# A hybrid decoder step on one core: page rows of 512 in two rings, chain loads one step ahead, operands of all products at equal places, and an end of its own for the last tile

## The chip, the core and the metric

The kernel runs on one core of a Trainium2 chip. The metric is the device time of one execution in microseconds (us). The engines are TensorE (PE in the rows of the profile, PEld for its weight loads), VectorE (DVE), ScalarE (ACT) and GpSimd (POOL); SyncE (SP) issues most of the DMAs. Matrices wait in SBUF, 128 partitions wide; TensorE writes its sums into PSUM. In a matmul one operand is loaded and stays (the stationary one, 128x128), the other streams through (the moving one, up to 512 columns).

## What is computed

One layer of a decoder over 16 meta tokens and 2048 prompt tokens, and over 8 running sequences of 4 tokens each. Two branches read the same projection: a diagonal state space layer (S5) and a gated DeltaNet (an attention with a matrix state, worked in chunks). Gates merge them, an output projection and a gated feed-forward layer follow, each with a norm and a residual. Cut to its core:

```python
hn = rms_norm(x, lp['norm_mix_pre'])
proj = hn @ lp['w_in']                                   # 1024 x 4616
u, qkv, z, a, bt, gates = jnp.split(proj, [o1, o2, o3, o4, o5], axis=-1)
y_s5, h_re_n, h_im_n = s5_mix(u, ...)                    # scan of a complex diagonal state
gs = jax.nn.gelu(y_s5)
br_a = (gs @ lp['w_s5_glu_a']) * jax.nn.sigmoid(gs @ lp['w_s5_glu_b'])
qkv_c, conv_new = short_conv(qkv, conv_buf, lp['gdn_conv_w'])
...
o_seg, S = gdn_segment(q, k, v, g, beta, S)              # chunks: decay, triangular solve, state
o = rms_norm(o, lp['gdn_norm']) * jax.nn.silu(zf)
br_b = o @ lp['w_gdn_out']
mix = (jax.nn.sigmoid(ga) * br_a + jax.nn.sigmoid(gb) * br_b) @ lp['w_out']
x = x + rms_norm(mix, lp['norm_mix_post'])
f = rms_norm(x, lp['norm_ffn_pre'])
f = (jax.nn.silu(f @ lp['w_ffn_gate']) * (f @ lp['w_ffn_up'])) @ lp['w_ffn_down']   # 1024 -> 2816 -> 1024
x = x + rms_norm(f, lp['norm_ffn_post'])
```

## The kernel before

All is float32. A product of two float32 matrices is made of three faster ones: each operand is split into a high and a low part (type fp32r), and `mm3` (L156 to L161) adds high x high, high x low and low x high, so every product is a run of three matmuls per 128 rows of the contraction.

The 2048 tokens stand in four blocks of 512; block 0 also carries the 16 meta tokens and the 32 sample tokens (560 columns, `PW`). The stages follow each other in time:

- **First stage** (`p1`, 0 to 1280 us of the page's span). `p1_features` loads the tokens of a block in tiles of 128, normalises them, transposes them on TensorE (`to_features`, `pst` at L252) and writes the features of the block, split in two, into *pages*: `pages(4)` takes four tiles of two rows for the high part (`pgh`) and four for the low one (`pgl`), each row 560 columns, out of one pool of 16 tiles. Blocks 0 and 1 form the first half, blocks 2 and 3 the second. In each half 36 units of 128 output columns of `w_in` (4 u, 12 qkv, 20 gates) multiply their weights (stationary, `wu`) with the pages (moving): `psq` and `psg`, eight rows of the contraction x three matmuls. Weights come through `wload` (L142 load, L144 high part on ScalarE, L146 and L147 low part, one half each on GpSimd and VectorE). Beside the units, by a count of ticks, run the S5 setup and groups, and the chunks of the DeltaNet: `gdn_alpha` loads a chunk's keys transposed (`kTa`, L584) and its decays (`E`, L562), multiplies keys with keys (`psk`, L590) and stores a chunk matrix (`m_d<-Z`, L607); all three tiles share three buffers (tag `al`). `gdn_chunk` solves and updates the state: `px` (L740) is a product of two times four small matmuls, with a copy to SBUF (`X`, L750) after each four; `o_out` normalises a chunk's output and transposes it (`pT`, L732). `s5_setup` loads the rows of the matrix C for half of the 32 groups (`ctl`, L1021) and transposes them (L1044).
- **Merge** (`merge`, 1280 to 1596): `p2_prep` multiplies and splits into pages again (two tiles for each of four lists), `p2_products` makes three products of each of 8 column tiles per block (`psgb`, `psga`, `psgo`; contraction of 4 rows).
- **Way out** (`way_out`, 1596 to 1800): the product with `w_out`. Here the merged rows (`hh`, and the low part) are stationary and the weights move; 17 tiles of tokens. The old rows x come into one pool of three buffers (`tm`).
- **Gate and up** (`gate_up`, 1800 to 2697): the two widest products (`psf`, 348 columns), untouched by the change.
- **Down** (`down`, 2697 to 3215): the product with `w_ffn_down`, in two halves of 8 token tiles, four groups of 5 or 6 weight tiles each. `hh` and `hl` (the split activations) are stationary, the weight tiles move (`psr` L1652 to L1655), sums are added up in `facc` (L1659). When the last group is done, a tile is normalised (Square on ScalarE L233, a root, a scaling L1666) and a GpSimd DMA adds it into `y_prompt` in memory (L1669), where the residual already stands.

Order: the program is Python that issues instructions in turn; a scheduler then lays them out in a fixed order for each engine, and each engine runs its own list from the front. A wait at the head of a list holds all behind it. SP's list holds nearly all loads and stores of a stage. Tiles of one tag share a fixed number of buffers: a new tile waits until the oldest is no longer read. Pools take their memory one after the other, from the left or the right end of SBUF, so a tile's size sets where the next pools' tiles start. The pool order of the down stage is `cv3`, `lw`, `hr`, `hh`, `ac3` from the left; `lw` has one buffer of 4096 bytes a partition.

What the edits touch in the text: `to_features` L243, `gdn_alpha` L573, `o_out` L711, `gdn_chunk` L737, `s5_setup` L881, `pages` L1246, `p2_prep` L1250, `way_rows` L1357, `down_tiles` L1630, the pools in `run` L1685, `p1_features` L1835.

## Time and profile before

| | us |
|---|---|
| time, median of 3 runs | 3237.43 (3235.34 to 3238.28) |
| the profiled execution | 3230.07 |
| its span in the profile | 3228.3 |
| first stage, its first half and its second | 0 to 722, 722 to 1280 |
| merge, way out | 1280 to 1596, 1596 to 1800 |
| gate and up, down, the end | 1800 to 2697, 2697 to 3215, 3215 to 3228 |
| mean granted clock of TensorE | 0.978 of full speed |

The profile is of one execution. A row of its timeline has the start and the duration of an instruction, the engine, the line, the operation, `out<-in` by the program's names and the shape; in brackets, how long the engine was idle ahead of it and what released it. A matmul's duration overlaps that of its neighbours, since matmuls are pipelined. A row of the waits has the engine, what it could not start, what released it, then the idle time in all, the number of waits and the longest. A row of a stretch of time has its length, busy time and number of instructions of each engine, the granted clock, the share of the DMA engines' time and GB/s. `issue` is idle time with no wait that the profile shows.

### The profile page before, as it was taken

What the parts mean: (1) busy time and instruction counts of PE and PEld (TensorE: products, weight loads), DVE (VectorE), ACT (ScalarE), POOL (GpSimd) and SP (SyncE); (2) the same over time, 40 slices, a digit from 0 to 9 for tenths busy, and PEclk for the clock granted to TensorE, in tenths of its full rate; (3) what the DMA queues carried; (4) which work ended last, traced back from release to release, by engine and by line L of the source; (5) the groups of instructions that cost most, each with busy time, mean ns of one, the idle gap of its engine ahead of it and who ended that gap; (6) DMA issues with size and microseconds to landing.
All of it is one profiled execution on the core that took longest, in us unless ns stands there. A gap on an engine that the chain in (4) does not pass through costs nothing.

```text
span 3228.3 us, 47504 instructions
## 1 busy us (share of the span) xinstructions
PE 3095.1 (96%) x17461; PEld 2719.5 (84%) x17461; DVE 2047.1 (63%) x4674; ACT 1127.2 (35%) x1952; POOL 892.9 (28%) x907
## 2 busy tenths in 40 slices
PE   7998989999999999899999899999999999999998
PEld 6887887877777887888788799999999998887776
DVE  6888864557798645644456777777777773245235
ACT  4642222433333224311244444444444444223211
POOL 1133431113332211300211444434434444121110
PEclk9999998999999999999999999999999999999999
DMA  4335556445556645544555533343323335235214
GB/s 120 122 98 164 137 157 179 116 111 141 158 172 180 169 120 149 173 132 134 162 175 190 171 105 105 105 123 106 105 88 105 105 105 174 83 107 133 88 57 70
DMA packets 460552, 419.29 MB, mean 130 GB/s; under 512 B 112330, under 2 KB 384906, under 8 KB 460320
## 3 DMA queue, kind: packets, MB, share of 16 engines
q1 hardware_dynamic: 450048, 382.18, 40.6%
q0 software_dynamic: 10272, 34.09, 3.8%
q8 instruction: 137, 2.24, 0.3%
q14 instruction: 95, 0.78, 0.1%
HBM read 288.27 MB, written 127.65 MB: 129 GB/s over the span
## 4 chain that ended last, share of the span: by engine, by line
PE 67%; DVE 15%; issue 10%; DMA 5%; ACT 2%; POOL 1%; SPq 0%; POOLq 0%; DVEq 0%; ACTq 0%
PE psf L161 9%; PE psf L159 9%; PE psf L160 9%; PE psr L1652 3%; PE psr L1653 3%; PE psr L1655 2%; PE psg L159 2%; PE psg L161 2%; PE psg L160 2%; DVE cy L391 2%; PE psr L1377 2%; PE psr L1378 2%; PE psr L1380 1%; PE psq L159 1%; PE psq L161 1%
## 5 line engine op out<-in xcount | busy, mean ns | idle before, releaser
L159 PE MATMUL psf<-xh,ah 128*128 128x348 f32 (+1 forms) x1848 | 595.0, 322 | 6.2 <-ACT sn L1546 4.5
L160 PE MATMUL psf<-xl,ah 128*128 128x348 f32 (+1 forms) x1848 | 593.8, 321 | 0.0
L161 PE MATMUL psf<-xh,al 128*128 128x348 f32 (+1 forms) x1848 | 593.5, 321 | 0.0
L146 POOL TENSOR_TENSOR wu<-wr,wu 128x512 fp32r<-128x512 f32 x136 | 218.1, 1606 | 690.0 <-ACT wu L144 664.1
L159 PEld LDWEIGHTS psf<-xh,ah 128*128 128x128 f32 x1848 | 348.3, 188 | 8.0 <-ACT sn L1546 5.4
L161 PEld LDWEIGHTS psf<-xh,al 128*128 128x128 f32 x1848 | 348.4, 189 | 0.2 <-DVE al L1486 0.2
L160 PEld LDWEIGHTS psf<-xl,ah 128*128 128x128 f32 x1848 | 348.4, 189 | 0.0
L159 PE MATMUL psg<-pgh,wu 128*128 128x512 f32 (+2 forms) x800 | 301.2, 377 | 1.2 <-ACT gt L1223 1.2
L1652 PE MATMUL psr<-wu,hh 128*128 128x512 f32 (+2 forms) x748 | 295.9, 396 | 3.9 <-ACT hh L1638 3.9
L1653 PE MATMUL psr<-wu,hh 128*128 128x512 f32 (+2 forms) x748 | 295.8, 395 | 0.0
L161 PE MATMUL psg<-pgh,wu 128*128 128x512 f32 (+2 forms) x800 | 290.3, 363 | 4.0 <-DVE wu L147 4.0
L160 PE MATMUL psg<-pgl,wu 128*128 128x512 f32 (+2 forms) x800 | 289.2, 362 | 0.0
L1655 PE MATMUL psr<-wu,hl 128*128 128x512 f32 x704 | 277.3, 395 | 0.0
L147 DVE TENSOR_TENSOR wu<-wr,wu 128x512 fp32r<-128x512 f32 x136 | 121.0, 891 | 130.7 <-ACT wu L144 127.8
L144 ACT ACTIVATE wu<-wr 128x1024 fp32r<-128x1024 f32 x136 | 142.6, 1054 | 133.8 <-DMA wr<-w_ffn_down 48.8
L159 PE MATMUL psq<-pgh,wu 128*128 128x512 f32 (+2 forms) x480 | 183.1, 381 | 4.6 <-ACT gt L1223 4.0
L161 PEld LDWEIGHTS psg<-pgh,wu 128*128 128x128 f32 x800 | 156.0, 195 | 28.7 <-DVE wu L147 4.2
L159 PEld LDWEIGHTS psg<-pgh,wu 128*128 128x128 f32 x800 | 155.8, 195 | 26.6 <-issue 6.1
L160 PE MATMUL psq<-pgl,wu 128*128 128x512 f32 (+2 forms) x480 | 174.4, 363 | 0.0
L161 PE MATMUL psq<-pgh,wu 128*128 128x512 f32 (+2 forms) x480 | 173.7, 362 | 0.0
L1652 PEld LDWEIGHTS psr<-wu,hh 128*128 128x128 f32 (+2 forms) x748 | 138.8, 186 | 39.8 <-ACT hh L1638 4.2
L160 PEld LDWEIGHTS psg<-pgl,wu 128*128 128x128 f32 x800 | 155.9, 195 | 19.2 <-issue 0.2
(498 smaller groups left out, 6721.3 us busy)
## 6 DMA issues: line engine op xcount, KB each, us to landing
wr<-w_in SPq DMA_DIRECT2D x72, 512.0 KB
araw<-w_ffn_gate SPq DMA_DIRECT2D x31, 1024.0 KB
araw<-w_ffn_up SPq DMA_DIRECT2D x31, 1024.0 KB
wr<-w_ffn_down SPq DMA_DIRECT2D x44, 512.0 KB
zg_d<-gt SPq DMA_DIRECT2D x80, 256.0 KB
h_d<-hm SPq DMA_DIRECT2D x44, 348.0 KB
qkv_d<-cy SPq DMA_DIRECT2D x48, 256.0 KB
hr<-h_d SPq DMA_DIRECT2D x16, 768.0 KB
```

Source lines behind the costliest of these rows:

```text
L144: nc.scalar.activation(hi[:, :n], raw[:, :n], AF.Copy)
L146: nc.gpsimd.tensor_sub(lo[:, :c], raw[:, :c], hi[:, :c].bitcast(F32))
L147: nc.vector.tensor_sub(lo[:, c:n], raw[:, c:n], hi[:, c:n].bitcast(F32))
L159: t.matmul(ps, wh, xh, start=first, stop=False, **kw)
L160: t.matmul(ps, wh, xl, start=False, stop=False, **kw)
L161: t.matmul(ps, wl, xh, start=False, stop=last, **kw)
L391: nc.vector.scalar_tensor_tensor(yp, raw[:, j:j + np_], w[j], yp, op0=OP.mult, op1=OP.add)
L1377: nc.tensor.matmul(o, hi[:, k, :rr], wh[:, cs], start=i == 0, stop=False)
L1378: nc.tensor.matmul(o, hi[:, k, :rr], wl[:, cs], start=False, stop=wide and i == 7)
L1652: nc.tensor.matmul(ps, hi[:, k, cl], wh[:, cs], start=k == 0, stop=False)
L1653: nc.tensor.matmul(ps, hi[:, k, cl], wl[:, cs], start=False, stop=both and k == n - 1)
L1655: nc.tensor.matmul(ps, lo[:, k, c - c0:c - c0 + r], wh[:, cs], start=False, stop=k == n - 1)
```

## The change

- **Pages.** One block's pages are now units of eight rows: a unit for the high part and one for the low part in the first stage; in the merge both parts of a list stand in one unit. There are two rings (`pg0` for even blocks, `pg1` for odd ones) of two units each. A row has 512 columns (2048 bytes), in block 0 it has 576 (`PITCH`, 2304 bytes); before, every row had 560 (2240 bytes).
- **First tokens.** In block 0, `to_features` takes three of its four PSUM tiles from the pool `gp` in place of `pt`.
- **Loads ahead.** `gdn_alpha` issues a chunk's `kTa` and `E` one chunk earlier; the tag `al` has five buffers in place of three. `s5_setup` issues the rows of C earlier (`rows_c`), into a buffer of the token tiles `tm` in place of `cv`.
- **Small moves.** `px`: both copies now come behind all eight matmuls. `o_out`: one more step of the count ahead of `pT`. The way out's x tiles go to three tags in a fixed turn, one buffer each. The down stage's twelve weight buffers come from two pools of six.
- **Operand places.** `lows`, in `lw`, has 96 columns more (4480 bytes for 4096), so all that lies behind it in the down stage (`hr`, `hh`, `ac`) starts 384 bytes later modulo 512.
- **The end.** The last prompt tile of the down stage has a path of its own (`down_end`): its residual is loaded ahead, the sum of squares and the scaling are made in two halves, and two plain SP stores write the result.

The diff, cut (line 41 adds `PITCH = 576`; `p1_features` passes `b == 0` as `wide`):

```diff
@@ -240,13 +241,14 @@
-    def to_features(self, ys, gain, hi, lo):
+    def to_features(self, ys, gain, hi, lo, wide):
 
         nc = self.nc
         c0 = ys[0][2]
         w = sum(r for _, r, _ in ys)
         for k0 in range(0, 8, 2):
-            ps = self.pt.tile([P, 2, 256], F32, tag="pt", name="pst")
+            pool, tag = (self.gp, "gp") if wide and k0 else (self.pt, "pt")
@@ -578,11 +580,15 @@
         v.memset(ssk, 1.0)
-        zs = []
+        new = lambda nm: self.gd.tile([P, H, P], F32, tag="al", bufs=5, name=nm)
+        def load(ci, nt, c0):
+            kT = new("kTa")[:, :, :nt]
+            nc.sync.dma_start(kT, ap_of(self.qkv_d, 512 * QW + c0, [[QW, P], [P * QW, H], [1, nt]]))
+            return kT, self.decay_load(ci, nt, new("E"))
+        nxt = load(*ch[0])
         for i, (ci, nt, c0) in enumerate(ch):
-            kT = self.gd.tile([P, H, P], F32, tag="al", bufs=3, name="kTa")[:, :, :nt]
-            nc.sync.dma_start(kT, ap_of(self.qkv_d, 512 * QW + c0, [[QW, P], [P * QW, H], [1, nt]]))
-            e = self.decay_load(ci, nt, self.gd.tile([P, H, P], F32, tag="al", bufs=3, name="E"))
+            kT, e = nxt
+            nxt = load(*ch[i + 1]) if i + 1 < n else None
@@ -592,7 +598,7 @@
-            z = self.gd.tile([P, H, P], F32, tag="al", bufs=3, name="Z")[:nt, :, :nt]
+            z = new("Z")[:nt, :, :nt]
@@ -726,6 +732,7 @@
         yield
+        yield
         pT = self.gp.tile([P, H, P], F32, tag="gp", name="pT")
@@ -747,6 +754,7 @@
                 mm(px[a:a + 32, h, 0:32], M[a + 32:a + 64, h, a:a + 32], V[a + 32:a + 64, h])
+        for a in (0, 64):
             v.tensor_copy(X[a:a + 32], px[a:a + 32, :, 0:32])
@@ -998,6 +1006,13 @@
 
         nc.sync.dma_start(ld[:16], ap_of(io["s5_D"], 0, [[1, 16], [16, G]]))
+        def rows_c(h0):
+            t = self.tm.tile([P, D], F32, tag="tm", name="ctl")[:, :512].rearrange("p (i q k e) -> p i q k e", i=2, q=2, k=2)
+            for i, nm in enumerate(("s5_C_re", "s5_C_im")):
+                for k in range(2):
+                    nc.sync.dma_start(t[:, i, :, k], ap_of(io[nm], h0 * 16 * 64, [[64, P], [P * 64, 2], [1, 64]]))
+            return [t[:, i] for i in range(2)]
+        nxt = rows_c(0)
 
@@ -1014,12 +1029,7 @@
             for d, nm in ((Br, "s5_B_re"), (Bi, "s5_B_im")):
                 for sl in (lo, hi):
                     nc.sync.dma_start(d[sl], io[nm].rearrange("o g p c -> p (o g) c")[:, h0:h0 + 16])
-            cts = []
-            for nm in ("s5_C_re", "s5_C_im"):
-                ct = self.c2("ctl")[:, :256].rearrange("p (q k e) -> p q k e", q=2, k=2)
-                for k in range(2):
-                    nc.sync.dma_start(ct[:, :, k], ap_of(io[nm], h0 * 16 * 64, [[64, P], [P * 64, 2], [1, 64]]))
-                cts.append(ct)
+            cts = nxt
@@ -1071,6 +1081,8 @@
                 outer(V2, (CR, CI), (R2, R1), "n", 1, 9)
+                if g0 == 12:
+                    nxt = rows_c(16)
                 nc.sync.dma_start(self.wv_d[gs, :, 3].rearrange("g p (t c) -> p g t c", c=16), V2)
@@ -1243,16 +1255,26 @@
 
-    def pages(self, n):
-        new = lambda nm: [self.pg.tile([P, 2, PW], F32R, tag="pg", name=nm) for _ in range(n)]
-        return new("pgh"), new("pgl")
+    def pages(self, b, n):
+
+
+        pitch = PITCH if b == 0 else BLK
+        out = []
+        for nm in ("pgh", "pgl"):
+            if n == 4 or nm == "pgh":
+                t = self.pg.tile([P, 8 * (PITCH if b % 2 == 0 else BLK)], F32R, tag=f"pg{b % 2}", bufs=2, name=nm)
+                rows = t[:, :8 * pitch].rearrange("p (k c) -> p k c", k=8)
+                at = 0
+            out.append([rows[:, at + 2 * i:at + 2 * i + 2] for i in range(n)])
+            at += 2 * n
+        return out
 
     def p2_prep(self, b):
 
         nc, v = self.nc, self.nc.vector
         width = BLK + SMP if b == 0 else BLK
 
-        oh, ol = self.pages(2)
+        oh, ol = self.pages(b, 2)
@@ -1364,7 +1386,8 @@
-        x = self.tm.tile([P, D], F32, tag="tm", name="xr")
+        n = c // P + 1 if c < SEQ else 0
+        x = self.tm.tile([P, D], F32, tag=f"tm{n % 3}", name="xr")
@@ -1645,6 +1669,9 @@
             cl = slice(c - c0, c - c0 + rr)
+            if gi == last and c + r == SEQ:
+                end = self.down_end(a, r, c)
+                next(end)
             for half in range(2):
@@ -1657,16 +1684,42 @@
                     v.tensor_add(a[:rr, cs], a[:rr, cs], ps)
+                if end:
+                    next(end)
             if wide and gi == last - 1:
-                t = self.lw.tile([SMP, D], F32, tag="lw", name="lows")
+                t = self.lw.tile([SMP, D + 96], F32, tag="lw", name="lows")[:, :D]
                 nc.sync.dma_start(t, a[r:2 * r])
                 nc.gpsimd.tensor_add(a[:r], a[:r], t)
-            if gi == last:
+            if gi == last and not end:
                 rs = self.rstd_of([(a, r, c)], "f")
                 v.scalar_tensor_tensor(a[:r], a[:r], rs[:r, 0:1], self.r_fpost[:r], op0=OP.mult, op1=OP.mult)
                 dst = (ap_of(self.io["y_prompt"], c * D, [[D, r], [1, D]]) if c < SEQ
                        else ap_of(self.io["y_sample"], 0, [[D, r], [1, D]]))
                 nc.gpsimd.dma_start(dst, a[:r], accum_op=OP.add)
+
+    def down_end(self, a, r, c):
+
+        nc, v = self.nc, self.nc.vector
+        rows = lambda cs: ap_of(self.io["y_prompt"], c * D + cs.start, [[D, r], [1, cs.stop - cs.start]])
+        halves = [slice(0, BLK), slice(BLK, D)]
+        y = self.lw.tile([P, D + 96], F32, tag="lw", name="yl")[:, :D]
+        nc.sync.dma_start(y, rows(slice(0, D)))
+        g = self.ac.tile([P, D], F32, tag="ac", name="fg")
+        ss = self.small.tile([P, 2], F32, tag="sse", bufs=1, name="sse")
+        rs = self.small.tile([P, 1], F32, tag="rse", bufs=1, name="rse")
+        yield
+        for i, cs in enumerate(halves):
+            j = self.c2("sq").bitcast(BF16)[:, :BLK]
+            nc.scalar.activation(j, a[:, cs], AF.Square, accum_out=ss[:, i:i + 1])
+            v.tensor_mul(g[:, cs], a[:, cs], self.r_fpost[:, cs])
+            if i == 0:
+                yield
+        v.tensor_add(ss[:, 0:1], ss[:, 0:1], ss[:, 1:2])
+        self.rsqrt(rs, ss[:, 0:1], 1.0 / D, EPS, "e")
+        for cs in halves:
+            v.scalar_tensor_tensor(g[:, cs], g[:, cs], rs[:, 0:1], y[:, cs], op0=OP.mult, op1=OP.add)
+            nc.sync.dma_start(rows(cs), g[:, cs])
+        yield
@@ -1703,7 +1756,7 @@
-                self.pg = self.pool("pg", 16, pgx, side="right")
+                self.pg = self.pool("pg", 2, pgx, side="right")
@@ -1726,7 +1779,7 @@
-                self.tm = self.pool("tm2", 3, ph, **kw)
+                self.tm = self.pool("tm2", 1, ph, **kw)
@@ -1758,7 +1811,8 @@
-            self.wp.add(self.pool("wp3", 12, ph, side="right", **kw), 12)
+            self.wp.add(self.pool("wp3", 6, ph, side="right", **kw), 6)
+            self.wp.add(self.pool("wp5", 6, ph, side="right", **kw), 6)
```

The scheduler lays out the new program anew, and in the first stage the rows of most engines have moved. Three places follow, each a piece of one engine's list before and after. Line numbers are those of the respective program (L584 is L586 after, L562 is L564, L607 is L613, L740 is L747, L159 to L161 are L160 to L162).

SP in the first stage, around the first full chunks of the DeltaNet, before. `kTa` and `E` are a chunk's loads, `m_d<-Z` its store, `zg_d<-gt` the store of a gate unit, `ctl` the rows of C, `wr<-w_in` the load of a weight tile:

```order
L1021 DMA ctl<-s_C_re 128x2x64 x2
L1021 DMA ctl<-s_C_im 128x2x64 x2
L1228 DMA zg_d<-gt 128x512
L607 DMA m_d<-Z 256x1x64
L1229 DMA zg_d<-gt 128x32
L584 DMA kTa<-qkv_d 128x4x128
L562 DMA E<-gct_d 128x512
L1231 DMA zg_d<-gt 128x512
L1068 DMA wv_d<-V 128x4x128
L142 DMA wr<-w_in 128x8x128 x2
```

The same place after:

```order
L1240 DMA zg_d<-gt 128x512
L1241 DMA zg_d<-gt 128x32
L586 DMA kTa<-qkv_d 128x4x128
L613 DMA m_d<-Z 256x1x64
L564 DMA E<-gct_d 128x512
L1243 DMA zg_d<-gt 128x512
L143 DMA wr<-w_in 128x8x128
L1078 DMA wv_d<-V 128x4x128
L586 DMA kTa<-qkv_d 128x4x128
L564 DMA E<-gct_d 128x512
L613 DMA m_d<-Z 128x512
```

Each chunk's loads now stand ahead of the store of the chunk before it, and the loads of C are gone from here. They stand near the front of SP's list, behind the stores of zeros (`L336`), ahead of the first store of a conv output (`qkv_d<-cy`), after:

```order
L218 DMA xt<-x_prompt 128x1024
L333 DMA u_d<-zero 128x4x8 x5
L336 DMA qkv_d<-zero 128x16 x12
L1013 DMA ctl<-s_C_re 128x2x64 x2
L1013 DMA ctl<-s_C_im 128x2x64 x2
L406 DMA qkv_d<-cy 128x16
L407 DMA qkv_d<-cy 128x32
L408 DMA qkv_d<-cy 128x512
```

TensorE in the first half, at the first chunk's `px` product (between the matmuls of a gate unit), before:

```order
L160 MATMUL psg<-pgl,wu 128x304
L740 MATMUL px<-U_5599,M 32x32 x4
L161 MATMUL psg<-pgh,wu 128x304
L159 MATMUL psg<-pgh,wu 128x304
L160 MATMUL psg<-pgl,wu 128x304
L161 MATMUL psg<-pgh,wu 128x304
L740 MATMUL px<-U_5599,M 32x32 x4
```

After:

```order
L160 MATMUL psg<-pgh,wu 128x304
L161 MATMUL psg<-pgl,wu 128x304
L747 MATMUL px<-U_5585,M 32x32 x8
L162 MATMUL psg<-pgh,wu 128x304
L160 MATMUL psg<-pgh,wu 128x304
L161 MATMUL psg<-pgl,wu 128x304
```

The two fours of `px`, four gate matmuls apart before, now stand together.

9 lines of the change are left out of this document (6 added, 3 removed).

## The prediction

> **What bounds the kernel now.** I read the page first, then busy time and clock by stage, the matmuls of single stretches in order of time, and PE's waits.
>
> ```profile
> span 3228.3 us, 47504 instructions
> PE 3095.1 (96%) x17461; PEld 2719.5 (84%) x17461; DVE 2047.1 (63%) x4674; ACT 1127.2 (35%) x1952; POOL 892.9 (28%) x907
> PE 67%; DVE 15%; issue 10%; DMA 5%; ACT 2%; POOL 1%; SPq 0%; POOLq 0%; DVEq 0%; ACTq 0%
> ```
>
> TensorE is busy nearly throughout and carries two thirds of the chain, so there are two ways to gain: matmuls that follow each other faster, and fewer waits of PE. The next rows give, by stretch, its length, then busy time (and count) of PE, weight loads, DVE, ACT and POOL, granted clock, DMA share and GB/s: the start, the first pass with the S5 setup, the second pass, the way out, and the down projection.
>
> ```profile
> 0.00:135.00 135.00, 110.64 (x636) 97.82 (x637) 102.68 (x356) 76.43 (x140) 17.46 (x22) 0.95 0.42 118
> 135.00:430.00 295.00, 266.98 (x1624) 235.42 (x1622) 246.69 (x853) 100.03 (x191) 107.85 (x121) 0.95 0.47 133
> 722.00:1020.00 298.00, 287.56 (x1369) 231.88 (x1368) 242.56 (x769) 96.47 (x191) 94.69 (x182) 0.98 0.56 160
> 1596.00:1800.00 204.00, 200.66 (x940) 162.52 (x941) 123.50 (x306) 85.51 (x157) 36.35 (x52) 1.00 0.55 181
> 2697.00:3215.00 518.00, 515.14 (x2210) 411.25 (x2210) 209.68 (x389) 123.63 (x143) 88.45 (x59) 1.00 0.38 102
> ```
>
> In the down projection PE never waits, so its time is its number of matmuls times their spacing. In the first 430 us PE is idle for 52 us in all, and VectorE is busy for 349 of 430: there a wait of PE may hide a VectorE that is nearly as late.
>
> **The matmuls' spacing.** A row's own duration (0.39 us) overlaps its neighbours', so I take starts. All these matmuls are 128x512, at full granted clock. Way out, first and last of 19 that follow each other; then the down projection (52), the merge (25) and the last gates of the first stage (11):
>
> ```profile
> 1678.77 0.39 PE L1377 MATMUL psr<-wu,hh 128*128 128x512 f32 x1
> ...
> 1682.85 0.39 PE L1377 MATMUL psr<-wu,hh 128*128 128x512 f32 x1
> ```
>
> ```profile
> 2907.01 0.39 PE L1652 MATMUL psr<-wu,hh 128*128 128x512 f32 x1
> ...
> 2918.86 0.39 PE L1652 MATMUL psr<-wu,hh 128*128 128x512 f32 x1
> ```
>
> ```profile
> 1459.91 0.39 PE L159 MATMUL psgo<-pgh,wu 128*128 128x512 f32 x1
> ...
> 1465.46 0.39 PE L159 MATMUL psga<-pgh,wu 128*128 128x512 f32 x1
> ```
>
> ```profile
> 1245.24 0.39 PE L160 MATMUL psg<-pgl,wu 128*128 128x512 f32 x1
> ...
> 1247.55 0.39 PE L161 MATMUL psg<-pgh,wu 128*128 128x512 f32 x1
> ```
>
> That is 4.08 us over 18 steps or 226.7 ns in the way out, 11.85 over 51 or 232.4 ns in the down projection, 5.55 over 24 or 231.3 ns in the merge, 2.31 over 10 or 231.0 ns in the gates. The way out and the down projection run the same three products in the same order. What differs in the built program is where the operands start: in the way out moving and stationary tiles both lie at 480 bytes modulo 512; in the down projection the moving weights lie at 480 and the stationary tiles at 96; in the merge and the first stage the stationary ones lie at 480 and the moving page rows wander, row by row, by 192 or 448 bytes modulo 512. The change puts all of them at 480, but for the odd rows of the first block (224). I read the 226.7 ns as the price of equal places.
>
> - Down: 2210 matmuls x 5.7 ns = 12.6 us. Nothing else stands on that path, so all of it counts.
> - Merge: blocks 1 to 3, 8 columns x 3 products x 4 k x 3 matmuls each = 864, x 4.6 ns = 4.0 us. All of it counts, since PE is the bound here too.
> - First stage: 36 units x 3 blocks x 24 = 2592, x 4.3 ns = 11.1 us. I count 6: in half of this stage VectorE is over 80% busy, and a PE that arrives sooner waits there. The narrower matmuls of the first block (256 to 304 columns) I count at nothing.
>
> Sum 22.6 us, bounds 0 (places do nothing) and 27.7.
>
> The Trainium skill, "SBUF — State Buffer", in "SBUF: two separate sides", says that of the engines' ports only the pair that VectorE and GpSimd share can contend, and that PE never waits on anyone; "TensorE: Matmul & The Clock Gate" adds, in the step on LDWEIGHTS, that loading the next weights takes no read bandwidth from the running matmul. By that these 22.6 us would be zero. The two spacings above, 226.7 and 232.4 ns, are not explained by it. The same TensorE page, under "Back-to-back issue gap", puts 512 columns at N / 2.4 + 2.5, some 216 ns; by it the down projection alone could give 36 us, but no stretch here shows less than 226.7.
>
> **The waits.** PE's waits, each with its total, how often, and the longest; the last row but one is VectorE's, the last SyncE's.
>
> ```profile
> PE pst L252 <- DVE xt L241: 19.1, 3, 13.3
> PE psk L590 <- DMA kTa<-qkv_d: 9.5, 1, 9.5
> PE px L740 <- DVE X L750: 9.1, 7, 3.1
> PE pT L732 <- DVE o L726: 8.7, 4, 6.0
> PE pst L1044 <- DMA ctl<-s_C_re: 6.0, 2, 4.2
> PE pst L1044 <- DMA ctl<-s_C_im: 5.2, 2, 4.9
> PE pst L252 <- issue: 4.8, 1, 4.8
> PE psr L1652 <- ACT hh L1638: 3.9, 1, 3.9
> DVE E L569 <- DMA E<-gct_d: 14.4, 12, 3.2
> SPq L584 <- PE psk L590: 0.5, 1, 0.5
> ```
>
> - C rows (L1021 before, rows_c after): loads now stand further ahead in SP's order, the first half's by some ninety instructions, the second half's by some 25. 6.0 + 5.2 = 11.2 us of waits go; I count 9, since POOL's products for the same step come next.
> - kTa one chunk ahead, five buffers for three: the 9.5 us wait goes; I count 8. After it PE also ran at half clock for 10 us: the row below (length, PE busy and count, clock, DMA) shows 22 matmuls in 10 us. I count 2 more for that.
>
> ```profile
> 300.00:310.00 10.00, 5.10 (x22) 0.50 0.76 231
> ```
>
> - E one chunk ahead: VectorE's 14.4 us over both passes. Where VectorE is 81% busy (722 to 1020) some of it reaches PE: 3, bounds 0 and 7.
> - Start: of the 19.1 us, 13.3 are the first tokens, which no edit touches. The other 5.8, and the 4.8 of "issue" (transposes that stand behind two PSUM tiles and behind the last tokens' load), meet five tiles instead of two and a load that SP now issues earlier. Of 10.6 I count 5: VectorE (103 of 135 us) is next late.
> - px: all eight matmuls now come ahead of the two copies, so the second four no longer wait for the first copy. Of 9.1 I count 6.
> - The additional step ahead of pT: 6.0 of the 8.7 us belong to the last chunk, whose transposes still follow its last product directly in the new order. Of the other 2.7 I count 1.5.
> - Down's first tiles: the first six weight tiles now lie at the right end, over memory that gate and up leave early. Of 3.9 I count 3.
> - The end, by the rows below: VectorE's last addition of a half, Square of the whole row, the first and the last step of the root, and the accumulating store, which takes 5.4 us to land.
>
> ```profile
> 3214.86 0.69 DVE L1659 TENSOR_TENSOR facc<-facc,psr 128x512 f32<-128x512 f32 x1 [0.93 <-PE psr L1655]
> 3215.64 1.06 ACT L233 ACTIVATE sq<-facc 128x1024 bf16<-128x1024 f32 x1 [5.82 <-DVE facc L1659]
> 3216.82 0.15 DVE L102 TENSOR_SCALAR rsx<-ss 128x1 f32<-128x1 f32 x1 [1.27 <-ACT sq L233]
> 3219.14 1.28 DVE L1666 SCALAR_TENSOR_TENSOR facc<-facc,rs,row 128x1024 f32<-128x1024 f32 x1
> 3220.71 0.86 POOL L1669 DMA_DIRECT2D y_prompt<-facc  x1 [5.64 <-DVE facc L1666]
> y_prompt<-facc POOLq DMA_DIRECT2D x4, 512.0 KB, 5.4
> 96.27 2.12 DMA zg_d<-gt
> ```
>
> From the end of that addition (3215.55) to landing (3226.1) it takes 10.6 us. After the change: half a Square with its hand-over (0.9), the sum of two (0.2), the root (3219.14 - 3216.82 = 2.3), two halves of the scaling (1.4), issue (0.4) and a plain store of 256 KB, for which the chain shows 2.12 in the first stage (zg_d): 7.3. Gain 3.2, counted 3. The y load it needs stands on SP well ahead.
>
> Sum of the waits: 9 + 8 + 2 + 3 + 5 + 6 + 1.5 + 3 + 3 = 40.5 us. Bounds: 10 (down's start, the end, little else) and 60 (every wait named, 7 of VectorE's).
>
> Against it stands the new static order. Every queue runs in the order in which it was built, and that has moved almost everywhere in the first stage. A token buffer is held for C rows, and SP's loads ahead stand before weight loads. The nearest price is a wait of PE on something moved past it, such as these two:
>
> ```profile
> PE pst L1099 <- DVE W L1060: 4.1, 1, 4.1
> PE psg L161 <- DVE wu L147: 4.0, 1, 4.0
> ```
>
> I take two new ones of this kind, 8 us (bounds 0 and 20).
>
> Total: 22.6 + 40.5 - 8.1 = 55.0 us. The profiled execution took 3230.07 us (span 3228.3 and 1.8 around it), so it would come to 3175.1. It lies 7.4 below the median of the three runs, 3237.43; I take the same 55.0 off the median: **3182.4 us**.
>
> **The rivals.**
>
> *Operand places do nothing.* The spacing then comes from other things that differ between the stages. For it: the traces show no run of one stage at two places. Against it: the way out moves more data than the down projection (181 against 102 GB/s), has a busier VectorE (123.50 of 204 us against 209.68 of 518), and is still the faster. Then only the waits go: 40.5 - 8.1 = 32.4, 3205 us. Chance 0.10; it is also what the skill's two rules give.
>
> *The first stage waits elsewhere.* VectorE, busy 349 of the first 430 us, is really the one that is late, and PE waits for it where it now waits for DMA. Then down (12.6), merge (4.0), down's start (3) and the end (3) remain: 22.6, 3215 us. For it: the 81%; against it: the two longest waits are named as DMA's, with nothing of VectorE's behind them. Chance 0.11.
>
> *Slower: loads ahead hold SP.* SP issues in order. A kTa or E load that is placed ahead of the release of its buffer stops SP, and behind it stand the weight loads and the stores of the first stage; PE then waits for weights. There are 13 such chunks (17 less the first of each block). Before, SP lost 0.5 us at L584 in the row above. It decides from 55.0 + 6.5 = 61.5 us, or 4.7 us of PE's time a chunk; with 6 a chunk it costs 78, and the time is 3237.4 - 55 + 78 = 3260 us. Five buffers for three speak against it, and that one chunk's tiles are read long before the next but one is asked for. Chance 0.03.
>
> **How the numbers follow.** The forecast has 0.76, the rivals 0.10, 0.11 and 0.03. The range must hold the forecast's own bounds and reach to the two milder rivals: low from 27.7 + 60 - 6 = 81.7 us of gain, 3156; high at the second rival, 3215. A difference of 0.2% (6.5 us) is about what a measurement of this kernel tells from none. Forecast and the two mild rivals all lie beyond it: faster 0.95, and 0.02 for within 0.2% (the second rival and the 20 us of new waits together), slower 0.03.
>
> **What would show it.** In the profile of the changed kernel: 128x512 matmuls of the down projection, of merge blocks 1 to 3 and of the first stage's blocks 1 to 3 starting every 227 ns, with down's 2210 in some 502 us; no row of PE waiting for kTa or for ctl; px's wait under 3 us; no half clock near 300 us; two plain stores at the end. The forecast is wrong if the down projection keeps its 232 ns (first rival), if PE's idle time in the first 430 us stays near 52 us under VectorE's name (second), or if PE waits for w_in loads while SP waits at L586 or L564 (third).

## The result, and the profile after

The changed kernel takes 3186.4 us (median of four runs, 3184.19 to 3188.53) against 3236.39 us before (3235.02 to 3238.28): a ratio of 0.9845, interval 0.9828 to 0.9862, or 50.0 us less. The forecast was 3182.4, or 55.0 less. The profiled execution took 3184.19 us.

The page of the changed kernel, the lines that answer to those of before:

```profile
span 3182.4 us, 47491 instructions
PE 3056.5 (96%) x17461; PEld 2707.1 (85%) x17461; DVE 2049.3 (64%) x4678; ACT 1129.2 (35%) x1956; POOL 896.4 (28%) x906
PE 75%; DVE 16%; DMA 4%; issue 2%; ACT 2%; POOL 1%; SPq 1%; DVEq 0%; ACTq 0%; POOLq 0%
```

PE's busy time fell by 38.6 us (3095.1 to 3056.5) with the same 17461 matmuls, and what lies outside it by 7.3 (span 133.2 to 125.9). A pipelined PE is also counted busy in many short waits, so this is no split into causes; it only says that the matmuls as a whole stand closer. Part of it is the clock: the mean granted clock rose from 0.978 to 0.982. In the two traces the stretches at half clock (0.50) add up to 141.6 us before and 117.3 after; half of the time that PE was busy in them comes to 53 and 43 us, so by this estimate some 10 of the 46 us between the two profiles are time at half clock that is gone.

Stretches of the changed kernel, in the columns of before: the first pass with the S5 setup, the rest of the first pass, the down projection, the merge.

```profile
135.00:430.00 295.00, 261.91 (x1601) 231.78 (x1600) 243.11 (x846) 101.10 (x191) 113.48 (x126) 0.95 0.47 132
430.00:722.00 292.00, 284.29 (x1990) 240.72 (x1989) 158.40 (x477) 95.97 (x242) 53.84 (x79) 0.95 0.57 148
...
2672.00:3173.00 501.00, 501.00 (x2209) 408.38 (x2209) 210.31 (x385) 120.10 (x141) 84.82 (x55) 1.00 0.38 102
1266.00:1571.00 305.00, 293.73 (x1691) 256.43 (x1689) 162.57 (x291) 72.04 (x120) 56.66 (x65) 0.99 0.52 155
```

The down projection's matmuls now fill 501 us. VectorE is busy for 82% of the first of these stretches and for 54% of the second; that difference will matter below.

The spacing, first and last of 53 matmuls of the down projection and of 46 in the merge's blocks 1 to 3:

```profile
2874.62 0.39 PE L1679 MATMUL psr<-wu,hh 128*128 128x512 f32 x1
...
2886.41 0.39 PE L1680 MATMUL psr<-wu,hh 128*128 128x512 f32 x1
```

```profile
1429.77 0.39 PE L160 MATMUL psgo<-pgh,wu 128*128 128x512 f32 x1
...
1439.97 0.39 PE L160 MATMUL psgb<-pgh,wu 128*128 128x512 f32 x1
```

11.79 us over 52 steps and 10.20 over 45: 226.7 ns in both, for 232.4 and 231.3 before.

PE's waits after:

```profile
PE pst L254 <- DVE xt L242: 21.8, 6, 13.7
PE pT L739 <- DVE o L732: 10.6, 4, 6.0
PE psq L160 <- ACT gt L1235: 9.3, 4, 5.8
PE psk L596 <- DMA kTa<-qkv_d: 9.2, 1, 9.2
...
PE pw L1159 <- DVE Z L602: 6.2, 2, 3.8
PE psg L160 <- ACT gt L1235: 6.1, 2, 5.8
...
PE psr L1679 <- ACT hh L1662: 2.0, 1, 2.0
```

The rows for `ctl` and the row for `px` behind `X` are gone, as forecast. The wait for `kTa` is still there, 9.2 us for 9.5, and so is the half clock at it: in the columns of the prediction's row for 300 to 310 us (length, PE busy and count, clock, DMA), ten microseconds there now read

```profile
295.00:305.00 10.00, 4.01 (x19) 0.52 0.62 169
```

`pT`'s wait has grown, 10.6 us for 8.7. And PE's waits for ScalarE's `gt`, of which the largest rows were 4.0 and 1.2 us before, have come to 15.4.

PE's idle time in the first 430 us has not fallen. It was 52.4 us by the prediction's first two stretches (24.4 and 28.0); now it is 430 - 373.6 = 56.4, for nearly the same number of matmuls (2260 and 2262):

```profile
0.00:430.00 430.00, 373.60 (x2262) 332.58 (x2263) 350.44 (x1217) 180.14 (x335) 131.54 (x148) 0.95 0.47 131
```

By landmarks of the two traces (first fp32r product of each stage), in us:

```
                      before    after
first matmul starts     13.3     13.7    +0.4
first stage           1267.7   1251.9   -15.8
merge                  315.3    305.5    -9.8
way out                201.7    201.8    +0.1
gate and up            901.6    898.9    -2.7
down                   514.8    501.3   -13.5
behind the last matmul  13.9      9.3    -4.6
```

The end, from the last addition of sums to the stores:

```profile
3173.54 0.69 DVE L1686 TENSOR_TENSOR facc<-facc,psr 128x512 f32<-128x512 f32 x1 [0.23 <-PE psr L1682]
...
3174.33 0.63 ACT L1713 ACTIVATE sq<-facc 128x512 bf16<-128x512 f32 x1 [2.31 <-DVE facc L1686]
...
3175.08 0.16 DVE L1717 TENSOR_TENSOR sse<-sse 128x1 f32<-128x1 f32 x1
...
3177.59 1.42 DVE L1720 SCALAR_TENSOR_TENSOR fg<-fg,rse,yl 128x512 f32<-128x512 f32 x2
3178.38 1.01 SPq L1721 DMA_DIRECT2D y_prompt<-fg  x2
```

From the end of that addition (3174.23) to the end of the span it takes 8.2 us, for 12.8 before (3215.55 to 3228.3). Up to the end of the scaling it is 4.8 us for 4.9 before, so the two halves gain next to nothing there. Behind the scaling it is 3.4 us (3179.01 to 3182.4) for 7.9 (3220.42 to 3228.3): the gain is that of the store.

### The profile page after: what moved, and what is told of

It reads as the page before. It is cut to its first block, busy times and chain, and to the rows that moved or that the text cites. A ratio compares the mean times of both kernels' runs of the same rounds, so it can differ in the third digit from the quotient of the medians.

```text
span 3182.4 us, 47491 instructions
## 1 busy us (share of the span) xinstructions
PE 3056.5 (96%) x17461; PEld 2707.1 (85%) x17461; DVE 2049.3 (64%) x4678; ACT 1129.2 (35%) x1956; POOL 896.4 (28%) x906
## 4 chain that ended last, share of the span: by engine, by line
PE 75%; DVE 16%; DMA 4%; issue 2%; ACT 2%; POOL 1%; SPq 1%; DVEq 0%; ACTq 0%; POOLq 0%
PE psf L162 9%; PE psf L160 9%; PE psf L161 9%; PE psr L1679 5%; PE psr L1680 5%; PE psr L1682 5%; PE psg L160 2%; PE psg L162 2%; PE psg L161 2%; DVE cy L393 2%; PE psr L1400 2%; PE psr L1401 2%; PE psr L1403 1%; PE psq L160 1%; PE psq L161 1%
## 5 line engine op out<-in xcount | busy, mean ns | idle before, releaser
L160 PE MATMUL psf<-xh,ah 128*128 128x348 f32 (+1 forms) x1848 | 594.6, 322 | 6.6 <-ACT sn L1569 4.7
L161 PE MATMUL psf<-xl,ah 128*128 128x348 f32 (+1 forms) x1848 | 593.2, 321 | 0.0
L162 PE MATMUL psf<-xh,al 128*128 128x348 f32 (+1 forms) x1848 | 592.9, 321 | 0.0
L160 PEld LDWEIGHTS psf<-xh,ah 128*128 128x128 f32 x1848 | 348.0, 188 | 8.6 <-ACT sn L1569 6.3
L161 PEld LDWEIGHTS psf<-xl,ah 128*128 128x128 f32 x1848 | 348.0, 188 | 0.0
L162 PEld LDWEIGHTS psf<-xh,al 128*128 128x128 f32 x1848 | 347.9, 188 | 0.0
L160 PE MATMUL psg<-pgh,wu 128*128 128x512 f32 (+2 forms) x800 | 298.9, 374 | 13.2 <-ACT gt L1235 6.1
L162 PE MATMUL psg<-pgh,wu 128*128 128x512 f32 (+2 forms) x800 | 288.9, 361 | 4.6 <-DVE wu L148 3.7
L1679 PE MATMUL psr<-wu,hh 128*128 128x512 f32 (+2 forms) x748 | 291.3, 389 | 2.0 <-ACT hh L1662 2.0
L1680 PE MATMUL psr<-wu,hh 128*128 128x512 f32 (+2 forms) x748 | 291.2, 389 | 0.0
L161 PE MATMUL psg<-pgl,wu 128*128 128x512 f32 (+2 forms) x800 | 287.7, 360 | 0.0
L160 PE MATMUL psq<-pgh,wu 128*128 128x512 f32 (+2 forms) x480 | 180.9, 377 | 10.3 <-ACT gt L1235 9.3
L160 PEld LDWEIGHTS psg<-pgh,wu 128*128 128x128 f32 x800 | 156.2, 195 | 40.6 <-issue 7.9
L162 PEld LDWEIGHTS psg<-pgh,wu 128*128 128x128 f32 x800 | 156.0, 195 | 26.5 <-DVE wu L148 3.9
L161 PE MATMUL psq<-pgl,wu 128*128 128x512 f32 (+2 forms) x480 | 172.2, 359 | 2.4 <-DVE pgl L260 2.4
L1509 POOL TENSOR_TENSOR al<-R,ah 128x1024 fp32r<-128x1024 f32 x62 | 162.2, 2616 | 35.5 <-ACT ah L1508 31.6
L162 PE MATMUL psq<-pgh,wu 128*128 128x512 f32 (+2 forms) x480 | 172.1, 358 | 0.0
L161 PEld LDWEIGHTS psg<-pgl,wu 128*128 128x128 f32 x800 | 156.4, 195 | 17.7 <-issue 0.2
```

Of the source, the lines that this page charges most:

```text
L160: t.matmul(ps, wh, xh, start=first, stop=False, **kw)
L161: t.matmul(ps, wh, xl, start=False, stop=False, **kw)
L162: t.matmul(ps, wl, xh, start=False, stop=last, **kw)
L1509: eng.tensor_sub(flat(lo), x, flat(hi).bitcast(F32))
L1679: nc.tensor.matmul(ps, hi[:, k, cl], wh[:, cs], start=k == 0, stop=False)
L1680: nc.tensor.matmul(ps, hi[:, k, cl], wl[:, cs], start=False, stop=both and k == n - 1)
```

## The experiments

All medians below stand beside runs of the kernel before on the same chip (3235.0 to 3235.3 in the three groups); the changed kernel is taken at 3186.4.

```
                                            median    ratio to before, interval
changed kernel                              3186.40   0.9845  0.9828 to 0.9862
before, wider lows only                     3223.00   0.9963  0.9953 to 0.9974
before, pages and wider lows only           3211.02   0.9925  0.9912 to 0.9939
changed, four places (one run)              3194.58
changed, page rows of 560                   3207.80   0.9912  0.9898 to 0.9927
changed, block 2 alone at 560               3196.95   0.9876  0.9859 to 0.9892
  the same kernel again                     3194.87   0.9875  0.9861 to 0.9890
changed, no loads ahead in gdn_alpha        3186.70   0.9845  0.9829 to 0.9861
changed, C rows late                        3185.65   0.9846  0.9831 to 0.9860
changed, px, pT, first tokens undone        3205.98   0.9903  0.9888 to 0.9917
changed, block 1's first chunk ahead too    3182.82   0.9836  0.9822 to 0.9851
changed, no loads ahead, cv of 13           3181.66   0.9833  0.9818 to 0.9847
changed, first chunk ahead, cv of 12        3190.04   0.9866  0.9849 to 0.9883
```

A second view is used for several of them. The fp32r matmuls come in the same order in all these kernels up to the merge, and nearly so in it. So the start of the nth of them, from the first matmul of the trace on, can be compared between kernels. The table has the time in the changed kernel (of one profiled execution each), then how much later the same matmul starts in the others:

```
   nth  in the changed   before  places  small   C rows  seam   block 2  block 2
        kernel at                only    undone  late    load            again
   200     58.2            6.1     5.1     6.7     1.6     1.2    -0.5     0.4
  1100    214.2           12.3    11.4     6.6     9.3     1.4    -0.5     0.6
  1200    246.3            2.5     1.7     6.7     0.1     0.2     0.1     0.8
  1400    297.9            4.3     2.0     6.8    -0.6    -9.5     2.1     1.3
  1900    403.5           -1.1    -4.1     8.3    -7.5    -6.4     2.2     3.1
  2300    512.2            6.9     1.3     8.7    -1.3    -2.0     5.3     3.7
  2700    639.2           20.4    16.5    19.4    -0.3    -1.9     6.2     3.5
  3000    763.7           13.4     9.1    14.9    -0.4    -1.9     6.5     4.7
  3400    891.1           15.4     8.9    16.6     1.9    -2.1     9.3     5.4
  4400   1251.9           15.8     8.9    17.0     1.9    -4.2     8.0     6.1
  4500   1300.3           22.0    15.5    23.4     2.2    -4.6     9.2     7.5
  5900   1571.2           25.6    15.5    23.4     2.3    -4.6    10.5     8.9
```

Places only is "pages and wider lows only"; small undone is "px, pT, first tokens undone"; seam load is "block 1's first chunk ahead too". A column that falls gets time back; one that rises loses it there. Each column is one execution. How far it can be trusted, two profiles show whose programs are the same up to the down projection, the kernel before and "wider lows only": they differ by 3.5 us at the 4400th matmul and by 6.0 from the 4500th on, and by 2.2 in gate and up.

### Are the operand places the cause? The down projection alone

```diff
-                t = self.lw.tile([SMP, D], F32, tag="lw", name="lows")
+                t = self.lw.tile([SMP, D + 96], F32, tag="lw", name="lows")[:, :D]
```

> The kernel before with one line changed: lows is 96 columns wider, so hh and hl of the down projection start at 480 modulo 512 in place of 96, like the weights that move. Nothing else differs. Theory 'places' (the distance of the moving and the stationary operand modulo 512 bytes sets the spacing): the 2210 matmuls of the down projection start every 227 ns in place of 232.4, and the time falls by 12 to 13.5 us, to about 3223; all other stages as before. Rival 'not the places' (the spacing in the changed kernel comes from the pools of the weights, the schedule or the traffic): 232 ns and no change of the time.

Measured: 3223.0 us, 12.3 less than before, the order of every engine's instructions the same. Its down projection, by stretch and by the first and last of 53 matmuls:

```profile
2708.00:3211.00 503.00, 502.29 (x2205) 408.92 (x2206) 209.23 (x386) 122.13 (x142) 85.43 (x57) 1.00 0.38 104
```

```profile
2906.66 0.39 PE L1652 MATMUL psr<-wu,hh 128*128 128x512 f32 x1
...
2918.44 0.39 PE L1653 MATMUL psr<-wu,hh 128*128 128x512 f32 x1
```

11.78 us over 52 steps: 226.5 ns. What lies behind `lows` moved by 384 bytes, nothing else, and the time followed: the rival that places do nothing is out.

### Which places are equal? Four of them in one run

```diff
-        hi = self.hh.tile([P, 6, 256], F32R, tag="hh", name="hh")
+        hi = self.hh.tile([P, 6 * 256 + 32], F32R, tag="hh", name="hh")[:, :1536].rearrange("p (k c) -> p k c", k=6)
...
-            lo = self.hh.tile([P, 6, 256], F32R, tag="hl", name="hl")
+            lo = self.hh.tile([P, 6 * 256 + 32], F32R, tag="hl", name="hl")[:, :1536].rearrange("p (k c) -> p k c", k=6)
```

> The changed kernel with hh and hl of the down projection 32 columns (128 bytes) wider each, so their four buffers start at 480 and 96 (hh) and at 224 and 352 (hl) modulo 512; the weights still move from 480. One profile, read by the place of the stationary tile. Theory 'places, modulo 512': matmuls of hh at 480 start every 227 ns, those of the other three places every 231 to 236. Theory 'places, modulo 256': those at 224 also 227. Rival 'not the places': 227 ns at all four, and a down projection of 501 us as in the changed kernel; with the first theory about 7 us more.

Measured, mean ns to the next matmul's start, by the stationary tile's place of this matmul and of the next (the weights always move from 480; the places are those of the built program, and the rarer pairs are left out):

```
this -> next      count    ns         this -> next      count    ns
480 -> 480         396    227.5       96 -> 96           385    232.7
480 -> 224         261    227.1       96 -> 352          263    232.4
224 -> 480         254    226.9       352 -> 96          256    232.3
480 -> 352          88    232.6       224 -> 96          105    234.6
```

Its down projection took 509.2 us against 501.3. So 224 is as good as 480, and 96 and 352 are both worse, by 5 ns a matmul, as soon as one of the pair stands there: with the moving operand at 480, what counts is whether the stationary tile is equal to it modulo 256. "Modulo 512" was too narrow.

### The pages: rows of 560 again, then block 2 alone

```diff
-        pitch = PITCH if b == 0 else BLK
+        pitch = PW
...
-                t = self.pg.tile([P, 8 * (PITCH if b % 2 == 0 else BLK)], F32R, tag=f"pg{b % 2}", bufs=2, name=nm)
+                t = self.pg.tile([P, 8 * PW], F32R, tag=f"pg{b % 2}", bufs=2, name=nm)
```

> The changed kernel with page rows of 560 columns again, in its two rings of units, so the moving rows of the first stage and the merge wander by 192 bytes modulo 512; everything else as changed. Theory 'places': the merge's 512-wide matmuls start every 231 ns again and cost 4 us more, the first stage's 2592 every 231 in place of 228.4 and 4 to 7 us more, since part of it falls into waits; in all 8 to 11 us slower than the changed kernel, about 3196. Rival 'not the places': no change, 3186.

Measured: 3207.8, 21 us slower than the changed kernel, twice what the theory gave. The 512-wide spacing was as expected: 231.1 ns in the merge, 231.6 in the first stage. The rest is not explained by that spacing: the units are larger, so the pools behind them lie elsewhere, and the scheduler put the merge's preparation and the last chunk of the DeltaNet in another order at the seam (under a hundred of some 15000 rows on TensorE). Between the 4400th and the 4500th matmul alone this kernel loses 11.8 us. As a price of the places it is not usable, so the next one leaves sizes and order alone:

```diff
-        pitch = PITCH if b == 0 else BLK
+        pitch = PITCH if b == 0 else PW if b == 2 else BLK
```

> The changed kernel, but the rows of block 2 alone stand 560 columns apart in their units, so its moving rows wander by 192 bytes modulo 512; no instruction moves on any engine. Theory 'places': inside this one run the 512-wide matmuls of block 2 start every 231 ns (first stage 864 of them, merge 288), those of blocks 1 and 3 every 227 to 228; the time rises by 3 to 4 us. Rival 'not the places': all blocks alike and the time unchanged.

Inside this run the merge's matmuls of block 2 start every 231.1 ns on average, those of blocks 1 and 3 every 226.8. In the table the column rises by 1.3 us (9.2 to 10.5) across the merge's three wide blocks, about 288 x 4.3 ns, and by nothing else there. So the merge pays for places in full. In the second pass of the first stage, where 864 wider steps should add some 3 us, the column goes from 6.5 to 9.3 and back to 8.0: most of it is taken up by waits. But the kernel was 10.5 us slower, not 4, and in the profile 6.3 us of lag (the next expectation says 8) arose ahead of the first use of block 2, where no instruction and no operand place differs. So it ran once more:

> The same kernel as the run with block 2 alone at 560 columns, once more. That run came out 10 us slower than the changed kernel, of which the trace puts 8 ahead of the first use of block 2. If such a difference belongs to a loading of the program and not to the kernel, this one comes out near 3188, and the stretch ahead of block 2 as in the changed kernel; if it belongs to the kernel, 3197 again.

Measured: 3194.87, again slower by 8.5, with 3.5 of it ahead of block 2 in the profile. The longer time does belong to this kernel, then, and not to one loading of it. One stretch ahead of block 2 is alike in both profiles of this kernel: between the 2200th and the 2300th matmul each loses 4.8 us to the changed kernel. Here are 35 us of that stretch, in the changed kernel and then in the first run with block 2 at 560:

```profile
495.00:530.00 35.00, 35.00 (x161) 23.87 (x160) 19.57 (x60) 4.72 (x14) 5.20 (x4) 0.80 0.70 198
```

```profile
495.00:530.00 35.00, 35.00 (x114) 21.51 (x113) 17.27 (x53) 4.47 (x14) 3.81 (x4) 0.66 0.58 163
```

PE is busy throughout in both, but at a granted clock of 0.66 in place of 0.80 (0.66 in the second run too): 0.14 x 35, or 4.9 us by estimate, which is the loss. So about half of the surplus is time at half clock in this one place; why this kernel is granted less there, and what makes the rest, is open. It also says how small a difference of totals can be trusted in the first stage: below some 6 us not without its place in the trace.

### Places only

The kernel before with `pages`, its pools and calls, `PITCH` and the wider `lows` as changed:

```diff
-    def pages(self, n):
+    def pages(self, b, n):
...
-                self.pg = self.pool("pg", 16, pgx, side="right")
+                self.pg = self.pool("pg", 2, pgx, side="right")
...
+                t = self.lw.tile([SMP, D + 96], F32, tag="lw", name="lows")[:, :D]
```

> The kernel before with the change's page units (rows of 512, 576 in block 0, two rings) and the wider lows, and nothing else of the change. Forecast's terms: down 12.6, merge 4.0, first stage 6: about 3213. Theory 'places pay only where PE is late': the down projection and the merge gain 13 and 4 us, the first stage nothing, since waits take up what its matmuls gain: about 3219. Theory 'the pages bring more' (undoing them cost 21 us in the run with wandering rows): 12.5 and 21, about 3202.

Measured: 3211.0, 24.0 us less than before. Less the 12.3 of the down projection, 11.7 are the pages'. In the table this kernel leads the one before by 6.9 us at the merge's start (15.8 - 8.9), by 6.5 at the 4500th and by 10.1 at its end: 3.6 come across the merge's wide blocks. All the waits that the change aims at are still in it:

```profile
PE psk L591 <- DMA kTa<-qkv_d: 9.4, 1, 9.4
PE px L741 <- DVE X L751: 9.1, 7, 2.8
...
PE pst L1045 <- DMA ctl<-s_C_re: 6.4, 2, 4.7
...
PE pst L1045 <- DMA ctl<-s_C_im: 5.5, 2, 5.1
```

So the places are worth 24.0 and everything else of the change 24.6. In the first stage this kernel's order differs too, so the 6.9 there is the pages' as a whole.

### The loads ahead

```diff
-            kT, e = nxt
-            nxt = load(*ch[i + 1]) if i + 1 < n else None
+            kT, e = load(ci, nt, c0)
...
-        new = lambda nm: self.gd.tile([P, H, P], F32, tag="al", bufs=5, name=nm)
+        new = lambda nm: self.gd.tile([P, H, P], F32, tag="al", bufs=3, name=nm)
```

> The changed kernel, but gdn_alpha loads kTa and E of a chunk when it needs them, with three buffers, as before. Theory 'the seam': the only long wait for kTa, 9.2 us in the changed kernel as 9.5 before, belongs to the first chunk of block 1, whose load no chunk stands ahead of, so the loads ahead bought nothing there: between 2 us faster and 4 us slower than the changed kernel. Rival, as predicted: the loads ahead are worth 11 us (kTa 8, E 3), so 11 us slower, about 3197.

Measured: 3186.7, the same. PE did wait longer for `kTa` in it:

```profile
PE psk L594 <- DMA kTa<-qkv_d: 15.8, 3, 10.5
```

6.6 us more of waits at this place, and no more time in all. The long wait stays in both. In the changed kernel it is this one; the rows are SP's store of block 0's last chunk matrix, the next load of `kTa`, and the product that needs it:

```profile
297.07 0.32 SPq L613 DMA_DIRECT2D m_d<-Z  x1
...
297.92 0.45 SPq L586 DMA_DIRECT2D kTa<-qkv_d  x1
```

```profile
300.99 1.22 PE L596 MATMUL psk<-kTa 128*128 128x128 f32 x4 [9.23 <-DMA kTa<-qkv_d]
```

`gdn_alpha` runs once for a block. The first chunk of block 1 has no chunk of its own ahead of it; its load stands behind the store of block 0's last one, which waits for VectorE.

### The seam closed

```diff
-        nxt = load(*ch[0])
+        nxt = self.ahead or load(*ch[0])
+        self.ahead = None
...
+            if i + 1 == n and b % 2 == 0:
+                self.ahead = load(*self.chunks(b + 1)[0])
```

> The changed kernel, and gdn_alpha also loads the first chunk of the second block of each half ahead, beside the last chunk of the first. Theory 'the seam': the 9.2 us wait for kTa was that chunk's; it goes, with the half clock behind it (22 matmuls in some 10 us), and the time falls by 8 to 11 us. Rival 'given back': VectorE is nearly as late there, PE meets it at the next of its products, and the time falls by 0 to 3 us.

Measured: 3182.82, 3.6 less than the changed kernel. No row of PE names `kTa` any more, and at the 1400th matmul this kernel leads by 9.5 us (the 1200th: 0.2 behind). At the 2300th 2.0 are left. The waits that grew, from 2.3 and 3.7 us in the changed kernel:

```profile
PE psg L160 <- ACT raw L380: 10.9, 4, 3.7
...
PE psg L162 <- DVE wu L148: 6.5, 1, 6.5
```

Those for `gt` stayed, 14.4 us for 15.4. Both theories were half right: the wait was the seam's, and some seven of its nine or ten microseconds were given back within 220 us.

### The C rows

```diff
-            cts = nxt
+            cts = []
+            for nm in ("s5_C_re", "s5_C_im"):
+                ct = self.c2("ctl")[:, :256].rearrange("p (q k e) -> p q k e", q=2, k=2)
+                for k in range(2):
+                    nc.sync.dma_start(ct[:, :, k], ap_of(io[nm], h0 * 16 * 64, [[64, P], [P * 64, 2], [1, 64]]))
+                cts.append(ct)
```

> The changed kernel, but the rows of C are loaded where they are needed, into two buffers of the ring cv, as before. Forecast's theory: PE's two waits for ctl return (11.2 us in the kernel before) and the time rises by 9 us, to about 3195. Rival 'given back': the time that PE no longer lost to ctl it loses elsewhere in the changed kernel (its waits for gt rose from 5.8 to 16.2 us, since ScalarE's gt now finds its place in the ring cv occupied), so with the rows of C late again the waits for gt shrink as those for ctl return, and the time stays within 3 us of the changed kernel's.

Measured: 3185.65, the same as the changed kernel. The waits:

```profile
PE pst L1052 <- DMA ctl<-s_C_re: 11.6, 2, 7.2
...
PE psq L160 <- ACT gt L1231: 4.4, 2, 3.1
...
PE psg L160 <- ACT gt L1231: 0.9, 2, 0.7
```

12.4 us for `ctl` (0.8 of it for `s_C_im`) are back, and those for `gt` are 5.3 in place of 15.4. The table shows the exchange: 7.7 us lost between the 200th matmul (1.6) and the 1100th (9.3), 9.2 won back in the next hundred. The changed kernel pays there for this, PE's wait at 260 us:

```profile
260.06 0.58 PE L160 MATMUL psq<-pgh,wu 128*128 128x256 f32 x1 [5.81 <-ACT gt L1235]
```

and later for this one, in which ScalarE stands at a `gt` until VectorE is done with a tile W of the S5 setup:

```profile
407.54 0.70 ACT L1235 ACTIVATE gt<-psg 128x256 f32<-128x256 f32 x2 [15.70 <-DVE W L1070]
```

```profile
406.71 0.67 DVE L1070 TENSOR_TENSOR W<-W,ow 128x512 f32<-128x512 f32 x1
```

### The three small edits

```diff
-        for a in (0, 64):
-            v.tensor_copy(X[a:a + 32], px[a:a + 32, :, 0:32])
+            v.tensor_copy(X[a:a + 32], px[a:a + 32, :, 0:32])
...
-        yield
         pT = self.gp.tile([P, H, P], F32, tag="gp", name="pT")
...
-            yield from self.to_features(grp, self.g_mix, hi, lo, b == 0)
+            yield from self.to_features(grp, self.g_mix, hi, lo, False)
```

> The changed kernel with three small edits of the first stage undone: px's copies stand behind each four matmuls, one step less ahead of pT, and to_features takes all its tiles from the pool pt. Forecast's terms: px 6, pT 1.5, start 5, so 12.5 us slower than the changed kernel, about 3199. Rival 'given back': what PE no longer waits for here it waits for elsewhere in the first stage, and the time stays within 4 us of the changed kernel.

Measured: 3205.98, 19.6 us slower than the changed kernel: more than the forecast's 12.5, and not given back. The number is not a sharp one. Two of the five runs, at granted clocks of 0.982 and 0.983, were 12.4 and 12.9 us slower than the changed kernel's median; three, at 0.978 to 0.980, were 19.6 to 21.6. The profile is that of the slowest, the changed kernel's that of its fastest. The waits are there again:

```profile
PE px L746 <- DVE X L756: 8.6, 7, 2.5
...
PE pst L254 <- issue: 5.0, 1, 5.0
```

In the table 6.7 us are lost by the 200th matmul and never recovered: that is the first tokens' edit, since px and pT come much later. Between the 2300th and the 3000th 6.2 go, and 6.4 more at the seam to the merge, where the last chunk's small products stand among few others. Those 13 are put down to px and the step ahead of pT together; they were not told apart. At the seam it is hardly a matter of waits. Here is the way from the 4400th to the 4500th matmul in the changed kernel, then in this one:

```profile
1265.60:1314.00 48.40, 38.12 (x354) 34.86 (x353) 33.71 (x96) 22.20 (x50) 8.11 (x10) 0.93 0.59 155
```

```profile
1282.20:1337.10 54.90, 43.29 (x355) 39.60 (x354) 34.08 (x95) 21.37 (x48) 7.24 (x10) 0.84 0.50 134
```

Of the 6.5 us that it takes longer, 5.2 are time in which PE is busy, at a lower granted clock (0.84 for 0.93). Over the whole profiles the half clock costs this kernel 57 us of PE's time by the estimate made above, and the changed one 43: 14 of the 24 us between these two profiles. That the edits set the clock is not shown: the run without loads ahead, which has them, was at half clock at the seam for 17.1 us, as long as this one, and lost only 2.7 us there.

### Two more places in the ring, and both gains together

Three buffers in `al`, no loads ahead, and 13 places in `cv`:

```diff
-                    self.cv = self.pool("cv", 11, ph)
+                    self.cv = self.pool("cv", 13, ph)
```

> The changed kernel without the loads ahead of gdn_alpha (three buffers), and the ring cv, out of which gt and the tiles of the S5 setup come in turn, has 13 places in place of 11. Theory 'the ring': ScalarE's gt waits for a place that VectorE reads late; with two more places PE's waits for gt (16.2 us in the changed kernel) fall below 6, and the time falls by 5 to 10 us. Rival 'VectorE': what VectorE is late with, PE meets elsewhere, and the time stays within 3 us.

Measured: 3181.66, 4.7 less than the changed kernel. The waits for `gt` fell to 1.0 (with 0.8 and 0.4 for VectorE's part of it), those for `kTa` rose:

```profile
PE psk L594 <- DMA kTa<-qkv_d: 21.8, 7, 8.4
...
PE psq L160 <- ACT gt L1233: 1.0, 1, 1.0
```

14.4 us of waits for `gt` gone, 12.6 come back at `kTa` (6.6 of them already without the two places, in the run with no loads ahead), and 4.7 kept. Then the load across the seam with 12 places (four buffers in `al`):

> The changed kernel with the first chunk of a half's second block loaded ahead too, four buffers in al, and 12 places in the ring cv: the two edits that gained 3.6 and 4.7 us alone. If they add up: 8 us faster than the changed kernel, about 3178. If both only move PE's waits within the first stage, whose VectorE stays as late: 3 to 5 us faster, 3182.

Measured: 3190.0, 3.6 slower than the changed kernel: in this form, with 12 places and not 13 and with the loads ahead, the two gains do not add up. The waits stand elsewhere again:

```profile
PE psg L162 <- DVE wu L148: 7.7, 1, 7.7
PE py L1182 <- DVE sab L1166: 7.4, 2, 4.2
```

The lowest time measured is the one with 13 places and no loads ahead, 3181.66, below both kernels; its interval (0.9818 to 0.9847) overlaps the changed kernel's (0.9828 to 0.9862), so the 4.7 us are likely and not certain.

## Why the prediction came close, point by point

- **Down, 12.6 us:** right. 12.3 by the run that moves nothing but what lies behind `lows`, 226.5 ns for the 226.7 read from the way out. The two profiles have 13.5.
- **Merge, 4.0:** right. 3.8 across the wide blocks in the table (21.8 at the 4700th matmul, 25.6 at the end), 3.6 with places only, and 1.3 for block 2 alone. None of it was given back: PE is the bound there.
- **Places in the first stage, 6 of 11.1:** the size is right (6.9 for the pages, start of the merge), by another working. Its 512-wide spacing fell to 228.4 on average, not 227, so 2592 x 2.6 = 6.7 us were there to be had at all.
- **The Trainium skill on places:** by the two rules cited, "SBUF — State Buffer", "SBUF: two separate sides", and the LDWEIGHTS step of "TensorE: Matmul & The Clock Gate", no place could matter. The runs disagree: 12.3 us from the width of one tile, and 227 against 232.5 ns by the stationary tile's place within one run. The measurement decides.
- **kTa and E, 8 + 2 + 3:** wrong, 0 measured. The step that failed reads "kTa one chunk ahead, five buffers for three: the 9.5 us wait goes". It does not: the wait is that of block 1's first chunk, which the edit leaves where it was. The third rival even counted "17 less the first of each block". The half clock stayed with it, 0.52 in the ten microseconds from 295. And the 6.6 us that the loads ahead do take from the other chunks were given back.
- **C rows, 9:** the waits went, as forecast (11.2 us), and the time did not. "POOL's products for the same step come next" named the wrong follower: ScalarE's `gt` came next, behind VectorE.
- **px 6, pT 1.5, start 5:** right in kind for px and the start, and together too small by the medians: 19.6 for 12.5, with two of the five runs at 12.4 and 12.9. The start is 6.7; px with pT is 13 by the profile for 7.5, of which I had counted the waits at `px` and `pT` alone; the 6.4 at the seam to the merge I had left out, and 5.2 of the 6.5 us there are PE busy at a lower clock. Of pT's 1.5 no run shows anything: its wait went from 8.7 to 10.6 us, and is 8.5 with the edits undone.
- **Down's start, 3, and the end, 3:** the wait for `hh` fell from 3.9 to 2.0; the end gave 4.6. The norm in halves came out as added up (4.8 us to the end of the scaling; the sum had 0.9 + 0.2 + 2.3 + 1.4) and was hardly shorter than before. What was too small is the gain of the two plain stores: 3.4 us from the scaling to the end of the span, for 7.9.
- **New waits, 8 us (8.1 in the total):** the right sum under the wrong cover. PE's waits for ScalarE's `gt` rose from 5.2 to 15.4 us. I had taken that for disorder from the new schedule; it is where the C rows' gain went.

By the runs: places 24.0; small edits 19.6; end 4.6; down's start 1.9; loads ahead and C rows 0. That is 50.1, and the change measured 50.0. So close a sum is luck too: the 24.0 and the 19.6 are each known to some 4 or 5 us, and 4.6 and 1.9 are from one profile each. The forecast had 22.6, 12.5, 3, 3 and 22 for these, less 8.1. Its total was close because its errors offset each other: 22 us for waits that were worth nothing, against 8.1 taken off for disorder, 7.1 too little for the small edits and 1.9 too little for the rest. That is luck, not a right account of the first stage. The low end of the range, too, takes off 6 us for new waits, a number that follows from no bound given there (0 and 20).

The second rival, that PE is held by VectorE in the first stage, was right for one part of it. Its sign came: PE's idle time in the first 430 us stayed (52.4 us before, 56.4 after), though a good part of it stands under ScalarE's `gt`, with VectorE behind that. What was gained in the first 430 us behind the first tokens (C rows, kTa, E, the seam) was given back within some 200 us; there VectorE is busy for 82% of the time. What was gained between 512 and 764 us by the small edits (6.2 us net) was kept, and VectorE is busy for 54% from 430 to 722. That VectorE's share decides this fits these runs, but no run made VectorE faster by itself, and none held the granted clock fixed, so it is argued and not shown.
